# Reordering the first loads of a 64-unit time-mixing kernel: halves on two queues, three units in float32, and a later gate for the casting loads

## The chip, the cores and the metric

The kernel runs on one core of a Trainium2 chip. The metric is device time in microseconds (us) of one execution, lower is better. Each kernel is executed several times; a run with several rounds executes it alternately with the kernel before on the same chip. Medians are quoted. A profile records one execution; its span is about 1.7 to 2.1 us shorter than the time reported for it.

## The reference, cut to what matters

```python
x_prev = np.zeros_like(x); x_prev[:, 1:, :] = x[:, :-1, :]      # x is (16, 2048, 256) float32
xv = x * time_mix_v + x_prev * (1 - time_mix_v)                 # xr likewise; xk and k are not used
v = xv.reshape(-1, 256) @ value_weight
r = xr.reshape(-1, 256) @ receptance_weight
out = (sigmoid(r) * v) @ output_weight                          # float32
```

## The kernel before

The 32,768 rows are worked in 64 units of 512 rows, four units to a batch (of 2048 rows). For each unit TensorE transposes x (`ps_t`), ScalarE copies it to SBUF as bf16 (`xt`), VectorE and GpSimd multiply it by a coefficient per channel (`c_sb`) and VectorE adds the row ahead (`mix`), TensorE projects twice (`psum_r`, `psum_v`), ScalarE takes the sigmoid (`s_sb`), VectorE multiplies (`z_sb`), TensorE does the output product (`psum_o`) and ScalarE copies it out. The weights are multiplied once by `tms` so that the mix needs one product. Transposes run some units ahead, so the order is fixed: while unit 4 is worked on, units 7 and 8 (counted from 0) are transposed as a pair.

How x comes in: GpSimd issues loads that cast float32 to bf16 on the way (`x_bf`). They go through one queue in order. Only the first two units are loaded in float32 by the sync queue (`x_unit`), because that is sooner; they are transposed in float32. A dummy copy on GpSimd that reads a loaded tile is the gate that holds the casting loads back until that tile has landed:

```python
for m, tm in enumerate([time_mix_r, time_mix_v]):
    nc.scalar.dma_start(out=tm_rows[...], in_=...)
nc.scalar.dma_start(out=x_last, in_=rows(0)[:, J - 1, :])
for h in range(2):
    nc.sync.dma_start(out=x_unit[:, 0, h * H : (h + 1) * H], in_=...)
nc.sync.dma_start(out=w_f32[:, 0], in_=...)        # receptance weight
nc.sync.dma_start(out=x_unit[:, 1], in_=...)       # second unit
nc.sync.dma_start(out=w_f32[:, 1], in_=...)        # value weight
...
nc.gpsimd.tensor_copy(out=gate, in_=x_last[:, 0:1])          # gate
load(0, 2 * UJ, 3 * UJ)                                      # third unit, cast
nc.gpsimd.dma_start(out=wo_bf, in_=...)                      # output weight, cast
load(0, 3 * UJ, J)                                           # fourth unit
nc.gpsimd.tensor_copy(out=gate, in_=x_unit[:, 1, 0, 0:1])    # second gate
load(1, 3 * UJ, J); load(1, 0, UJ); load(1, UJ, 3 * UJ)      # second batch
load(2)                                                      # third batch, one load
```

Before the first data TensorE multiplies zeros (34 matmuls, `warm_up(WARM)`; 12 more later) so that its clock comes up: in the profile, four float32 transposes take 1.11 us at 4.93 us and 0.60 us at 6.27.

Of the kernel before, what the change touches and what calls it, by code (L numbers as in the profile page):

```python
# [8 lines left out]
FP32 = mybir.dt.float32  # L9
BF16 = mybir.dt.bfloat16  # L10
ALU = mybir.AluOpType
ACT = mybir.ActivationFunctionType
# [3 lines left out]
def kernel(  # L16
# [22 lines left out]
    nc = tc.nc  # L39

    B, S, D = x.shape
    P = 128
    KO = D // P
    J = S // P
    UJ = 4
    TU = UJ * P
# [3 lines left out]
    H = UJ // 2  # L50
    START_T = [1, 3, 5, 6, 8, 9, 11, 12]
    AHEAD = 6
    PAIRS = 12
    WARM = 34
    WARM2 = 12

    consts = ctx.enter_context(tc.tile_pool(name="consts", bufs=1))
    xpool = ctx.enter_context(tc.tile_pool(name="xpool", bufs=3))
# [4 lines left out]
    ps_t_pool = ctx.enter_context(tc.tile_pool(name="ps_t", bufs=2, space=bass.MemoryType.PSUM))  # L63
    ps_v_pool = ctx.enter_context(tc.tile_pool(name="ps_v", bufs=1, space=bass.MemoryType.PSUM))
    ps_r_pool = ctx.enter_context(tc.tile_pool(name="ps_r", bufs=1, space=bass.MemoryType.PSUM))
# [7 lines left out]
    xt = {}  # L73
    mix = {}
# [5 lines left out]
    ident_f = consts.tile([P, P], FP32)  # L80
# [4 lines left out]
    def rows(b):  # L85
        return x[b].rearrange("(p j) d -> p j d", p=P)

    def load(b, lo=0, hi=J):
        if b not in x_bf:
            x_bf[b] = xpool.tile([P, J, D], BF16, name="x_bf")  # L90
        nc.gpsimd.dma_start(out=x_bf[b][:, lo:hi, :], in_=rows(b)[:, lo:hi, :])  # L91

    x_last = consts.tile([P, D], FP32)
    x_unit = consts.tile([P, 2, UJ, D], FP32)
    tm_rows = consts.tile([2 * KO, P], FP32)
    w_f32 = consts.tile([P, 2, KO, D], FP32)
    for m, tm in enumerate([time_mix_r, time_mix_v]):
        nc.scalar.dma_start(  # L98
            out=tm_rows[m * KO : (m + 1) * KO, :], in_=tm.rearrange("(ko p) -> ko p", p=P)
        )  # L100
    nc.scalar.dma_start(out=x_last, in_=rows(0)[:, J - 1, :])
    for h in range(2):
        nc.sync.dma_start(
            out=x_unit[:, 0, h * H : (h + 1) * H], in_=rows(0)[:, h * H : (h + 1) * H, :]
        )
    nc.sync.dma_start(
        out=w_f32[:, 0], in_=receptance_weight.rearrange("(ko p) n -> p ko n", p=P)
    )
    nc.sync.dma_start(out=x_unit[:, 1], in_=rows(0)[:, UJ : 2 * UJ, :])
    nc.sync.dma_start(out=w_f32[:, 1], in_=value_weight.rearrange("(ko p) n -> p ko n", p=P))  # L110
    sig0 = consts.tile([P, 1], BF16)
    nc.scalar.activation(out=sig0, in_=zeros[:, 0:1], func=ACT.Sigmoid)  # L112
    w_bf = consts.tile([P, 2, KO, D], BF16)
    wo_bf = consts.tile([P, KO, D], BF16)
    gate = consts.tile([P, 1], FP32)
    nc.gpsimd.tensor_copy(out=gate, in_=x_last[:, 0:1])
    load(0, 2 * UJ, 3 * UJ)
    nc.gpsimd.dma_start(out=wo_bf, in_=output_weight.rearrange("(ko p) n -> p ko n", p=P))  # L118
    load(0, 3 * UJ, J)
    nc.gpsimd.tensor_copy(out=gate, in_=x_unit[:, 1, 0, 0:1])  # L120
    load(1, 3 * UJ, J)
    load(1, 0, UJ)
    load(1, UJ, 3 * UJ)
# [6 lines left out]

    warm_up(WARM)

# [5 lines left out]
    tms = consts.tile([P, 2, KO], FP32)  # L138
    c_sb = consts.tile([P, 2, KO], FP32)

    def coefficients():
        ps = ps_o_pool.tile([P, 2, KO], FP32, name="psum_o")
        nc.tensor.transpose(  # L143
            out=ps.rearrange("p m k -> p (m k)"), in_=tm_rows, identity=ident_f[: 2 * KO, : 2 * KO]
        )
        tm = consts.tile([P, 2, KO], FP32)
        nc.vector.tensor_copy(out=tm, in_=ps)  # L147
        nc.vector.tensor_scalar(
            out=tms, in0=tm, scalar1=0.0, scalar2=1e-30, op0=ALU.is_equal, op1=ALU.mult
        )  # L150
        nc.vector.tensor_tensor(out=tms, in0=tms, in1=tm, op=ALU.add)
        nc.vector.reciprocal(c_sb, tms)
        nc.vector.tensor_scalar(out=c_sb, in0=c_sb, scalar1=-1.0, scalar2=None, op0=ALU.add)

    coefficients()

    def transposes(i):

        b, e = divmod(i, UB)
        if b > 0:  # L160
            if e == 0:
                new_xt(b)
            e = (e - 1) % UB
        c0 = (1 + e * UJ) * P
        if i == 1:
            ps = ps_o_pool.tile([P, KO, TU], FP32, name="psum_o")
            src, idn = x_unit[:, 1], ident_f
        else:
            ps = ps_t_pool.tile([P, KO, TU], BF16, name="ps_t")
            src, idn = x_bf[b][:, e * UJ : (e + 1) * UJ, :], ident  # L170
        for ko in range(KO):
            for jj in range(UJ):
                nc.tensor.transpose(  # L173
                    out=ps[:, ko, jj * P : (jj + 1) * P],
                    in_=src[:, jj, ko * P : (ko + 1) * P],
                    identity=idn,
                )
        nc.scalar.copy(out=xt[b][:, :, c0 : c0 + TU], in_=ps)  # L178
        if e == UB - 1:
            late_copies.append(b)  # L180

    def first_transposes():
        def half(h, pool, name):
            ps = pool.tile([P, KO, TU], FP32, name=name)
            for ko in range(KO):
                for jj in range(H):
                    nc.tensor.transpose(  # L187
                        out=ps[:, ko, jj * P : (jj + 1) * P],
                        in_=x_unit[:, 0, h * H + jj, ko * P : (ko + 1) * P],
                        identity=ident_f,  # L190
                    )
            c0 = (1 + h * H) * P
            nc.scalar.copy(out=xt[0][:, :, c0 : c0 + H * P], in_=ps[:, :, 0 : H * P])  # L193

        half(0, ps_r_pool, "psum_r")
        pl = ps_t_pool.tile([P, KO, P], FP32, name="ps_t")
        for ko in range(KO):
            nc.tensor.transpose(
                out=pl[:, ko, 0:P], in_=x_last[:, ko * P : (ko + 1) * P], identity=ident_f
            )  # L200
        nc.vector.tensor_copy(out=xt[0][:, :, 1:P], in_=pl[:, :, 0 : P - 1])
        half(1, ps_v_pool, "psum_v")

    def scale(piece, kos=(0, 1)):
        b, m, lo, hi = piece
        for ko in kos:
            nc.vector.tensor_scalar(  # L207
                out=mix[b][:, m, ko, lo:hi],
                in0=xt[b][:, ko, lo:hi],
                scalar1=c_sb[:, m, ko : ko + 1],  # L210
                scalar2=None,
                op0=ALU.mult,
            )
# [13 lines left out]
    def add(piece):  # L227
        b, m, lo, hi = piece
        return nc.vector.tensor_tensor(  # L229
            out=mix[b][:, m, :, lo:hi],  # L230
            in0=mix[b][:, m, :, lo:hi],
            in1=xt[b][:, :, lo + P : hi + P],
            op=ALU.add,
        )
# [71 lines left out]
    def tile_for(b):  # L306
        if b not in mix:
            mix[b] = mixpool.tile([P, 2, KO, J * P], BF16, name="mix")

    def pieces(g):  # L310

        b, e = divmod(g, UB)
        tile_for(b)
        return [(b, m, e * TU, (e + 1) * TU) for m in range(2)]
# [16 lines left out]
    def advance(limit):  # L331
        nonlocal tnext
        while tnext <= min(limit, NU - 1):
            b, e = divmod(tnext, UB)
            if e == 1 and 2 < b + 2 < B:
                load(b + 2)
            transposes(tnext)
            tnext += 1

    first_transposes()  # L340
    tile_for(0)
    for h in range(2):
        half = (0, 0, h * H * P, (h + 1) * H * P)
        scale(half)
        add(half)
    for ko in range(KO):
        nc.scalar.activation(
            out=w_bf[:, 0, ko, :], in_=w_f32[:, 0, ko, :], func=ACT.Copy, scale=tms[:, 0, ko : ko + 1]
        )
    scale(pieces(0)[1])  # L350
    add(pieces(0)[1])
    for ko in range(KO):
        nc.vector.tensor_scalar(
            out=w_bf[:, 1, ko, :],
            in0=w_f32[:, 1, ko, :],
            scalar1=tms[:, 1, ko : ko + 1],
            scalar2=None,
            op0=ALU.mult,
        )
    warm_up(WARM2)  # L360
    advance(1)
    scale(pieces(1)[0])
    add(pieces(1)[0])

# [18 lines left out]
    for u in range(2, NU):  # L383
# [3 lines left out]
        for m, (b, _, lo, hi) in enumerate(pieces(u)):  # L387
            w = first[u][m]
# [3 lines left out]
                pooled[w - 1].append(group)  # L392
            else:
                products[w].append((group, (0, 1)))

    def scale_act(piece, kos):
        b, m, lo, hi = piece
        for ko in kos:
            nc.scalar.activation(  # L399
                out=mix[b][:, m, ko, lo:hi],  # L400
                in_=xt[b][:, ko, lo:hi],
                func=ACT.Copy,
                scale=c_sb[:, m, ko : ko + 1],
            )

    z_prev = None
    for g in range(NU - 1):
# [5 lines left out]
        for p in products.get(g + 1, []):  # L413
            if g + LOOK >= NU and p[0][1] == 1:
                scale_act(p[0], (0,))
# [57 lines left out]
```

## Time and profile before

| kernel before | |
|---|---|
| median | 213.88 us (213.71 to 214.05, 3 runs) |
| profiled execution | 214.59 us, span 212.8 us |
| busy share TensorE, VectorE, ScalarE, GpSimd | 95, 91, 88, 36 per cent |
| TensorE after 47 us | 3.04 us a unit, no gap |
| fourth unit's cast load | lands at 14.53 us |
| third batch's cast load | lands at 24.8 us |

The shares are averages over stages with different limits, and TensorE's says little about a change in the first 10 us. To value such a change one follows how its gain travels: the first units, then a stretch in which VectorE sets the pace (20 to 47 us), then one in which TensorE does.

### The profile page before, as it was taken

To read this page: it belongs to the slowest core of one execution; us is meant where nothing else is said; L and a number is where in the kernel's file an instruction comes from. 1 tells how busy PE (TensorE), PEld (TensorE's weight loads), DVE (VectorE), ACT (ScalarE), POOL (GpSimd) and SP (SyncE) were. 2 spreads that over 40 slices of the span, in tenths; PEclk is the share of its full clock that TensorE was granted. 3 is DMA by queue.
4 is the path that set the end of the run, shared out by engine and by line. 5 is a ranking of instruction groups with operands and counts; after the bars stand their busy time and mean duration, and the time that the engine had idled before them with its cause. 6 is when DMAs were issued, how large, how long until landed. Compare 5 with 4: busy or idle time off the path is not lost.

```text
span 212.8 us, 4177 instructions
## 1 busy us (share of the span) xinstructions
PE 202.0 (95%) x1566; PEld 134.9 (63%) x1593; DVE 193.8 (91%) x311; ACT 186.9 (88%) x202; POOL 77.1 (36%) x104
## 2 busy tenths in 40 slices
PE   8879999999999999999999999999999999999990
PEld 7537676666666666666666666666666666665570
DVE  1899999999999999999999999998999999999971
ACT  2688999998999999999999999999999999999870
POOL 1802331344453435434452444335343442344200
PEclk9999999999999999999999999999999999999998
DMA  5899999999969989998989999898989944443565
GB/s 181 196 176 216 240 288 285 326 234 337 245 152 288 277 228 339 176 348 179 291 243 225 340 200 354 157 325 211 260 283 216 354 200 197 197 172 162 208 249 200
DMA packets 9340, 51.91 MB, mean 244 GB/s; under 512 B 996, under 2 KB 1896, under 8 KB 3688
## 3 DMA queue, kind: packets, MB, share of 16 engines
q0 software_dynamic: 3008, 16.39, 43.9%
q1 hardware_dynamic: 6016, 34.87, 40.0%
q10 hardware_dynamic: 296, 0.40, 0.5%
q8 instruction: 12, 0.20, 0.3%
q14 instruction: 8, 0.07, 0.1%
HBM read 34.47 MB, written 33.55 MB: 320 GB/s over the span
## 4 chain that ended last, share of the span: by engine, by line
PE 73%; DVE 11%; DMA 5%; ACT 4%; issue 4%; POOL 1%; ACTq 0%; DVEq 0%
PE psum_o L250 22%; PE psum_v L240 20%; PE psum_r L240 19%; PE ps_t L173 10%; DVE z_sb L432 4%; DVE mix L229 3%; DMA x_bf<-in_x_dram 3%; DVE mix L207 2%; ACT s_sb L411 2%; DMA x_last<-in_x_dram 2%; ACT xt L178 1%; ACT o_sb L270 1%; PE ps_t L240 0%; ACTq L98 0%; POOL wo_bf L118 0%
## 5 line engine op out<-in xcount | busy, mean ns | idle before, releaser
L217 POOL TENSOR_SCALAR mix<-xt,c_sb 128x1024 bf16<-128x1024 bf16 (+1 forms) x61 | 64.4, 1057 | 117.0 <-DVE mix L229 101.4
L229 DVE TENSOR_TENSOR mix<-mix,xt 128x1024 bf16<-128x1024 bf16 (+1 forms) x129 | 90.0, 700 | 3.0 <-DVE mix L207 0.5
L432 DVE TENSOR_TENSOR z_sb<-s_sb,psum_v 128x1024 bf16<-128x1024 bf16 x63 | 76.6, 1216 | 4.8 <-PE psum_v L240 2.6
L270 ACT COPY o_sb<-psum_o 128x1024 f32<-128x1024 f32 x62 | 62.9, 1015 | 13.6 <-PE psum_o L250 13.2
L240 PEld LDWEIGHTS <-w_bf 128*128 128x128 bf16 x520 | 48.2, 98 | 35.4 <-issue 1.9
L240 PE MATMUL psum_v<-mix,w_bf 128*128 128x512 bf16 (+1 forms) x241 | 63.9, 377 | 1.7 <-DVE z_sb L432 0.6
L411 ACT ACTIVATE s_sb<-psum_r 128x1024 bf16<-128x1024 f32 x63 | 65.1, 1033 | 0.1
L250 PE MATMUL psum_o<-wo_bf,z_sb 128*128 128x256 bf16 x500 | 64.9, 273 | 0.2
L240 PE MATMUL psum_r<-mix,w_bf 128*128 128x512 bf16 (+1 forms) x244 | 64.0, 377 | 0.5
L178 ACT COPY xt<-ps_t 128x1024 bf16<-128x1024 bf16 x62 | 63.0, 1024 | 0.9 <-PE ps_t L173 0.9
L250 PEld LDWEIGHTS <-z_sb 128*128 128x128 bf16 x512 | 50.0, 98 | 19.1
L173 PEld LDWEIGHTS <-x_bf 128*128 128x128 bf16 x496 | 32.4, 98 | 15.6 <-DMA x_bf<-in_x_dram 2.4
L173 PE MATMUL ps_t<-ident,x_bf 128*128 128x128 bf16 x496 | 37.2, 219 | 1.6 <-DMA x_bf<-in_x_dram 1.4
L207 DVE TENSOR_SCALAR mix<-xt,c_sb 128x1024 bf16<-128x1024 bf16 (+2 forms) x89 | 35.5, 423 | 0.2
L91 POOL DMA_DIRECT2D x_bf<-in_x_dram x19 | 10.9, 577 | 0.0
L129 PE MATMUL ps_t<-zeros 128*128 128x128 bf16 x46 | 4.6, 289 | 1.0 <-DVE zeros L79 1.0
L129 PEld LDWEIGHTS <-zeros 128*128 128x128 bf16 x46 | 4.3, 135 | 1.0 <-DVE zeros L79 1.0
L399 ACT ACTIVATE mix<-xt,c_sb 128x512 bf16<-128x512 bf16 (+1 forms) x4 | 3.6, 930 | 0.0
L147 DVE COPY tm<-psum_o 128x4 f32<-128x4 f32 x1 | 0.2, 161 | 3.5 <-PE psum_o L143 3.5
L325 DVE COPY xt<-xt 128x254 bf16<-128x254 bf16 x15 | 3.3, 218 | 0.0
L112 ACT ACT_TABLE_LOAD x1 | 1.3, 1283 | 2.0 <-issue 2.0
L193 ACT CAST xt<-psum_r 128x512 bf16<-128x512 f32 x1 | 0.6, 585 | 2.5 <-PE psum_r L187 2.5
(45 smaller groups left out, 22.5 us busy)
## 6 DMA issues: line engine op xcount, KB each, us to landing
out_dram<-o_sb SPq DMA_DIRECT2D x30, 1024.0 KB, 7.1
x_bf<-in_x_dram POOLq DMA_DIRECT2D x14, 1024.0 KB, 10.8
x_bf<-in_x_dram POOLq DMA_DIRECT2D x4, 256.0 KB, 7.2
out_dram<-o_sb SPq DMA_DIRECT2D x2, 512.0 KB, 2.6
out_dram<-o_sb SPq DMA_DIRECT2D x3, 256.0 KB, 2.1
x_unit<-in_x_dram SPq DMA_DIRECT2D x2, 256.0 KB, 3.9
x_unit<-in_x_dram SPq DMA_DIRECT2D x1, 512.0 KB, 5.6
x_bf<-in_x_dram POOLq DMA_DIRECT2D x1, 512.0 KB, 10.9
```

The lines of the kernel that those rows point to most:

```text
L91: nc.gpsimd.dma_start(out=x_bf[b][:, lo:hi, :], in_=rows(b)[:, lo:hi, :])
L129: nc.tensor.matmul(out=ps, lhsT=zeros, rhs=zeros, start=True, stop=True)
L173: nc.tensor.transpose(out=ps[:, ko, jj * P : (jj + 1) * P], in_=src[:, jj, ko * P : (ko + 1) * P], identity=idn,)
L178: nc.scalar.copy(out=xt[b][:, :, c0 : c0 + TU], in_=ps)
L207: nc.vector.tensor_scalar(out=mix[b][:, m, ko, lo:hi], in0=xt[b][:, ko, lo:hi], scalar1=c_sb[:, m, ko : ko + 1], scalar2=None, op0=ALU.mult,)
L217: op = nc.gpsimd.tensor_scalar(out=mix[b][:, m, 1, lo:hi], in0=xt[b][:, 1, lo:hi], scalar1=c_sb[:, m, 1:2], scalar2=1.0, op0=ALU.mult, op1 ...
L229: return nc.vector.tensor_tensor(out=mix[b][:, m, :, lo:hi], in0=mix[b][:, m, :, lo:hi], in1=xt[b][:, :, lo + P : hi + P], op=ALU.add,)
L240: nc.tensor.matmul(out=ps[:, mo, :], lhsT=w_bf[:, m, ko, mo * P : (mo + 1) * P], rhs=mix[b][:, m, ko, e * TU + lo : e * TU + hi], start=(k ...
L250: nc.tensor.matmul(out=ps[:, slot, :], lhsT=z[:, ko, jj * P : (jj + 1) * P], rhs=wo_bf[:, ko, :], start=(ko == 0), stop=(ko == KO - 1),)
L270: nc.scalar.copy(out=o_sb[b][:, j0 : j0 + UJ, :], in_=ps)
L411: nc.scalar.activation(out=s_sb, in_=ps_r, func=ACT.Sigmoid)
L432: nc.vector.tensor_tensor(out=z_sb, in0=s_sb, in1=ps_v, op=ALU.mult)
```

## The change

Its intent is to have the first units ready sooner: the first unit's halves go out on two queues, the third unit comes in float32 through the faster queues too, the casting loads wait until the second unit has landed so that they don't compete with it, and work is moved between VectorE and ScalarE. Core of the diff:

```diff
-    WARM = 34
-    WARM2 = 12
+    WARM = 32
+    WARM2 = 10
...
+    load_unit(nc.sync, 0, 0, H)
+    load_unit(nc.scalar, 0, H, UJ)
     for m, tm in enumerate([time_mix_r, time_mix_v]):
-        nc.scalar.dma_start(
+        nc.sync.dma_start(
...
-    nc.gpsimd.tensor_copy(out=gate, in_=x_last[:, 0:1])
-    load(0, 2 * UJ, 3 * UJ)
+    load_unit(nc.sync, 2)                       # after the value weight
+    nc.gpsimd.tensor_copy(out=gate, in_=x_unit[:, 1, 0, 0:1])
+    load(0, 3 * UJ, J)
     nc.gpsimd.dma_start(out=wo_bf, ...)
-    load(0, 3 * UJ, J)
-    nc.gpsimd.tensor_copy(out=gate, in_=x_unit[:, 1, 0, 0:1])
...                                             # both weights scaled on ScalarE,
...                                             # half 1 copied by VectorE, x_last by ScalarE,
...                                             # unit 0 mixed whole, unit 2 transposed in float32
```

More of the change, by code (lines that the diff above doesn't have):

```diff
@@ L93, with load_unit, load_weight @@
     x_last = consts.tile([P, D], FP32)
-    x_unit = consts.tile([P, 2, UJ, D], FP32)
+    x_unit = consts.tile([P, 3, UJ, D], FP32)
     tm_rows = consts.tile([2 * KO, P], FP32)
     w_f32 = consts.tile([P, 2, KO, D], FP32)
+    def load_unit(queue, u, lo=0, hi=UJ):
+        queue.dma_start(out=x_unit[:, u, lo:hi], in_=rows(0)[:, u * UJ + lo : u * UJ + hi, :])
+    def load_weight(m, w):
+        nc.sync.dma_start(out=w_f32[:, m], in_=w.rearrange("(ko p) n -> p ko n", p=P))
+    load_unit(nc.sync, 0, 0, H)
+    load_unit(nc.scalar, 0, H, UJ)
     for m, tm in enumerate([time_mix_r, time_mix_v]):
-        nc.scalar.dma_start(
+        nc.sync.dma_start(
             out=tm_rows[m * KO : (m + 1) * KO, :], in_=tm.rearrange("(ko p) -> ko p", p=P)
@@ L101 @@
     nc.scalar.dma_start(out=x_last, in_=rows(0)[:, J - 1, :])
-    for h in range(2):
-        nc.sync.dma_start(
-            out=x_unit[:, 0, h * H : (h + 1) * H], in_=rows(0)[:, h * H : (h + 1) * H, :]
-        )
-    nc.sync.dma_start(
-        out=w_f32[:, 0], in_=receptance_weight.rearrange("(ko p) n -> p ko n", p=P)
-    )
-    nc.sync.dma_start(out=x_unit[:, 1], in_=rows(0)[:, UJ : 2 * UJ, :])
-    nc.sync.dma_start(out=w_f32[:, 1], in_=value_weight.rearrange("(ko p) n -> p ko n", p=P))
+    load_weight(0, receptance_weight)
+    load_unit(nc.sync, 1)
+    load_weight(1, value_weight)
+    load_unit(nc.sync, 2)
     sig0 = consts.tile([P, 1], BF16)
@@ L145, in coefficients @@
         )
-        tm = consts.tile([P, 2, KO], FP32)
-        nc.vector.tensor_copy(out=tm, in_=ps)
         nc.vector.tensor_scalar(
-            out=tms, in0=tm, scalar1=0.0, scalar2=1e-30, op0=ALU.is_equal, op1=ALU.mult
+            out=tms, in0=ps, scalar1=0.0, scalar2=1e-30, op0=ALU.is_equal, op1=ALU.mult
         )
-        nc.vector.tensor_tensor(out=tms, in0=tms, in1=tm, op=ALU.add)
+        nc.vector.tensor_tensor(out=tms, in0=tms, in1=ps, op=ALU.add)
         nc.vector.reciprocal(c_sb, tms)
         nc.vector.tensor_scalar(out=c_sb, in0=c_sb, scalar1=-1.0, scalar2=None, op0=ALU.add)
-    coefficients()
     def transposes(i):
@@ L164, in transposes, with one @@
         c0 = (1 + e * UJ) * P
+        def one(ps, ko, src, idn):
+            for jj in range(UJ):
+                nc.tensor.transpose(
+                    out=ps[:, jj * P : (jj + 1) * P],
+                    in_=src[:, jj, ko * P : (ko + 1) * P],
+                    identity=idn,
+                )
+        if i == 2:
+            for ko in range(KO):
+                ps = ps_t_pool.tile([P, TU], FP32, name="ps_t")
+                one(ps, ko, x_unit[:, i], ident_f)
+                nc.scalar.copy(out=xt[b][:, ko, c0 : c0 + TU], in_=ps)
+            return
         if i == 1:
             ps = ps_o_pool.tile([P, KO, TU], FP32, name="psum_o")
-            src, idn = x_unit[:, 1], ident_f
+            src, idn = x_unit[:, i], ident_f
         else:
@@ L171, in transposes @@
         for ko in range(KO):
-            for jj in range(UJ):
-                nc.tensor.transpose(
-                    out=ps[:, ko, jj * P : (jj + 1) * P],
-                    in_=src[:, jj, ko * P : (ko + 1) * P],
-                    identity=idn,
-                )
+            one(ps[:, ko], ko, src, idn)
         nc.scalar.copy(out=xt[b][:, :, c0 : c0 + TU], in_=ps)
@@ L182, in first_transposes @@
     def first_transposes():
-        def half(h, pool, name):
+        for h, (pool, name) in enumerate([(ps_r_pool, "psum_r"), (ps_v_pool, "psum_v")]):
             ps = pool.tile([P, KO, TU], FP32, name=name)
@@ L192, in half @@
             c0 = (1 + h * H) * P
-            nc.scalar.copy(out=xt[0][:, :, c0 : c0 + H * P], in_=ps[:, :, 0 : H * P])
-        half(0, ps_r_pool, "psum_r")
+            copy = nc.vector.tensor_copy if h else nc.scalar.copy
+            copy(out=xt[0][:, :, c0 : c0 + H * P], in_=ps[:, :, 0 : H * P])
+            if h == 0:
+                coefficients()
         pl = ps_t_pool.tile([P, KO, P], FP32, name="ps_t")
@@ L200, in first_transposes @@
             )
-        nc.vector.tensor_copy(out=xt[0][:, :, 1:P], in_=pl[:, :, 0 : P - 1])
-        half(1, ps_v_pool, "psum_v")
+        nc.scalar.copy(out=xt[0][:, :, 1:P], in_=pl[:, :, 0 : P - 1])
     def scale(piece, kos=(0, 1)):
@@ L338, in advance, with scale_act, weight_act @@
             tnext += 1
-    first_transposes()
-    tile_for(0)
-    for h in range(2):
-        half = (0, 0, h * H * P, (h + 1) * H * P)
-        scale(half)
-        add(half)
-    for ko in range(KO):
-        nc.scalar.activation(
-            out=w_bf[:, 0, ko, :], in_=w_f32[:, 0, ko, :], func=ACT.Copy, scale=tms[:, 0, ko : ko + 1]
-        )
-    scale(pieces(0)[1])
-    add(pieces(0)[1])
-    for ko in range(KO):
-        nc.vector.tensor_scalar(
-            out=w_bf[:, 1, ko, :],
-            in0=w_f32[:, 1, ko, :],
-            scalar1=tms[:, 1, ko : ko + 1],
-            scalar2=None,
-            op0=ALU.mult,
-        )
+    def scale_act(piece, kos):
+        b, m, lo, hi = piece
+        for ko in kos:
+            nc.scalar.activation(
+                out=mix[b][:, m, ko, lo:hi],
+                in_=xt[b][:, ko, lo:hi],
+                func=ACT.Copy,
+                scale=c_sb[:, m, ko : ko + 1],
+            )
+    def weight_act(m):
+        for ko in range(KO):
+            nc.scalar.activation(
+                out=w_bf[:, m, ko, :], in_=w_f32[:, m, ko, :], func=ACT.Copy, scale=tms[:, m, ko : ko + 1]
+            )
+    first_transposes()
+    unit0 = pieces(0)
+    weight_act(0)
+    scale(unit0[0])
+    scale(unit0[1], (0,))
+    add(unit0[0])
+    scale(unit0[1], (1,))
+    add(unit0[1])
     warm_up(WARM2)
     advance(1)
+    weight_act(1)
     scale(pieces(1)[0])
@@ L394 @@
                 products[w].append((group, (0, 1)))
-    def scale_act(piece, kos):
-        b, m, lo, hi = piece
-        for ko in kos:
-            nc.scalar.activation(
-                out=mix[b][:, m, ko, lo:hi],
-                in_=xt[b][:, ko, lo:hi],
-                func=ACT.Copy,
-                scale=c_sb[:, m, ko : ko + 1],
-            )
     z_prev = None
```

## The prediction

> **What bounds the kernel now.** I read the shares of the page first, then busy time by stage, then the chain of waits, and then the first 20 us in order of time. The columns of the stage table are the stretch, its length, busy us of each engine with instruction counts, the granted clock, the DMA share and GB/s:
>
> ```profile
> 0.00:10.00 10.00, 8.48 (x68) 6.98 (x69) 4.51 (x18) 4.46 (x7) 4.67 (x15) 1.00 0.69 194
> 10.00:20.00 10.00, 8.03 (x66) 4.93 (x67) 9.07 (x20) 8.24 (x11) 1.73 (x4) 1.00 1.08 189
> 20.00:47.00 27.00, 26.61 (x218) 17.80 (x221) 27.00 (x53) 26.11 (x29) 8.05 (x14) 1.00 1.02 268
> 47.00:205.00 158.00, 156.45 (x1197) 103.40 (x1218) 150.67 (x219) 146.06 (x155) 62.65 (x72) 1.00 0.83 248
> ```
>
> From 47 us on TensorE has no gap. The chain there is made of its groups alone: 0.86 + 0.86 + 0.87 + 0.45 = 3.04 us a unit. From 20 to 47 us VectorE is busy for all 27.00 us, TensorE and ScalarE nearly so; the chain runs through z_sb (L432), the adds (L229) and the products (L207). The change touches neither stretch: below the second unit its instruction lists are those of before. What it can do is start them earlier. A shift of VectorE at 20 us passes one for one to the end, because both stretches follow in order and TensorE has about 1.2 us of stalls to give between 16.8 and 48.4 us (29.15 us of groups in the 29.81 us between two r projections, then 0.56 us before L240 at 48.45). So the question is what sets the start. The chain of waits, in start, us, what:
>
> ```profile
> 1.59 4.35 DMA x_last<-in_x_dram
> 6.18 0.66 POOL x_bf L91
> 6.84 0.70 POOL wo_bf L118
> 7.55 6.98 DMA x_bf<-in_x_dram
> 14.58 0.62 PE ps_t L173 x8
> 15.20 0.86 PE psum_v L240 x4
> 16.06 0.89 PE psum_o L250 x8
> 16.97 1.01 ACT o_sb L270
> 17.98 0.92 ACT s_sb L411
> 18.91 1.83 ACT xt L178 x2
> ```
>
> x_last lands at 5.94 us and opens the cast loads; the fourth unit's cast load (third in the queue) lands at 14.53; TensorE, then ScalarE, carry that to 20.74 us, where VectorE takes over. The lines of the same time show the rest (start, us, engine, line, what, idle before and releaser):
>
> ```profile
> 7.90 1.06 PE L173 MATMUL psum_o<-ident_f,x_unit 128*128 128x128 f32 x8 [0.36 <-DMA x_unit<-in_x_dram]
> 9.07 1.02 PE L240 MATMUL psum_r<-mix,w_bf 128*128 128x512 bf16 x3
> 10.64 1.08 PE L240 MATMUL psum_v<-mix,w_bf 128*128 128x512 bf16 x4 [0.54 <-DVE w_bf L353]
> 12.20 0.62 PE L173 MATMUL ps_t<-ident,x_bf 128*128 128x128 bf16 x8 [0.49 <-DMA x_bf<-in_x_dram]
> 14.58 0.62 PE L173 MATMUL ps_t<-ident,x_bf 128*128 128x128 bf16 x8 [0.89 <-DMA x_bf<-in_x_dram]
> 16.17 1.22 DVE L432 TENSOR_TENSOR z_sb<-s_sb,psum_v 128x1024 bf16<-128x1024 bf16 x1 [0.53 <-PE psum_v L240]
> 19.66 1.22 DVE L432 TENSOR_TENSOR z_sb<-s_sb,psum_v 128x1024 bf16<-128x1024 bf16 x1 [0.28 <-PE psum_v L240]
> ```
>
> TensorE loses 2.49 us between 9.07 and 16.77 us (7.70 us, in which its groups need 5.21), on the second weight and two cast loads. But VectorE, the later bound, waits only 0.53 and 0.28 us. That caps the gain well below 2.49.
>
> **What the Trainium skill says.** "DMA: Bandwidth & Descriptors", section "Issuing engines are not separate DMA queues": queues of several engines share the 16 DMA engines, so a second issuer saves only issue time. The trace agrees in kind: the sync queue took 0.86 us for two halves; they landed 3.2 and 4.6 us after issue. The same page, "SWDGE vs HWDGE vs iDMA", says that a load that casts must be issued by GpSimd; that is why the change has to take the third unit in float32. Its section "Anatomy of one DMA" gives about 2.0 us of fixed time, mostly the receipt. The trace agrees: the cast queue had moved 0.655 MB, all through the fourth unit, by about 12.9 us, and that load landed at 14.53, 1.6 us later. "ScalarE: Activation LUTs", section "What ACT_TABLE_LOAD costs", gives 280 ns plus 0.833 ns a column with one pointer operand, and 93 ns of overlap back to back: 493 ns for 256 columns. The trace has 497 to 510, and 0.91 us for two.
>
> **The change part by part.** Times are of the new kernel, estimated from durations of the old trace.
>
> 1. Front. 32 warm matmuls at 112 ns instead of 34 end at about 4.6 us, not 4.8. The halves leave on two queues; the second lands near 4.5 instead of 5.8. Four first transposes at the cold pace of about 0.24 us a step run to 5.55. The coefficients follow (not first): matrix at 5.8, four small VectorE operations instead of five at 0.2 us, to 6.6. Half 1 is copied by VectorE: 254 columns from PSUM took 0.42 us and 1024 took 1.21, so 512 cost about 0.69, to 7.3. ScalarE copies half 0 to 6.25, the x_last columns to 7.25, and scales the r weight to 8.15. VectorE: two products and one of v, 0.9 us, the add 0.65: r mix ready at 8.85 (before: 8.92). The whole-unit products and adds cost 0.67 + 0.69 = 1.36 us where two halves cost 0.61 + 0.42 + 0.48 + 0.42 = 1.93, but 0.69 came in and 0.42 went: a wash. First projection 8.9 instead of 9.07.
>
> 2. Second unit. Its transposes wait for x_unit, which landed at 7.8. The bytes ahead in the queue are the same and start 0.4 us earlier, but two issues of time_mix stand ahead: 7.5 to 7.8 us. Its copy on ScalarE starts at 8.5 to 8.95; I use 8.95.
>
> 3. v weight on ScalarE: two at 0.41 us step, after that copy, so 9.9 to 10.7. v projection from 10.35, its second half at 10.75, as before; the sigmoid of unit 0 moves from 10.13 to 10.7 and ends 11.75. VectorE loses 0.67 us of work; z of unit 0 starts at 11.75 instead of 12.00, now behind the sigmoid.
>
> 4. Third unit in float32: eight transposes in 1.06 us instead of 0.62 and two copies at 0.585 instead of one of 1.01, both beside other work. Data at about 9 us (0.52 MB at 400 GB/s behind the rest). TensorE takes it straight after the v projection, at 11.5 to 12.6, instead of waiting to 12.20. ScalarE: scaled v of unit 1 11.65 to 12.97, copies 12.9 to 13.9, sigmoid of unit 1 to 14.9. VectorE: z to 12.95, add to 13.6, four products to 14.85, add to 15.5. z of unit 1 at 15.5 instead of 16.17; with the 1.14 + 2.07 us of work up to the next, z of unit 2 at 18.7 instead of 19.66. Gain so far 0.95 us.
>
> 5. Cast loads. The gate moves from 5.94 to about 7.7, but 0.26 MB of the old stream (unit 2) is gone and unit 3 goes first. First packets came 1.6 us after the issue: 9.4. The old stream moved 128 packets of 2 KB in about 1.8 us, then 256 short ones of the output weight in about 1.6: unit 3 moved at 11.2 and landed at 12.9 (before 14.53), output weight moved at 12.9. At 12.9 us the old stream stood at exactly this point, so everything behind lands as before. The DMA engines have no spare time there (share 1.08). Those landings: fifth and sixth unit about 16.0 and 17.3 (bytes moved by 14.3 and 15.7 us, plus the 1.6), third batch 24.8 us (issued 9.93, 14.9 us to landing).
>
> 6. So the gain meets the third batch. The ninth unit's transposes came second of a pair starting at 24.37, thus at 24.82 us, just as the data landed. A TensorE 0.95 us ahead must wait there; v of that step then ends at 24.8 + 0.45 + 0.86 + 0.1 = 26.2, and z, which ran at 26.49, moves by only 0.25 to 0.3 us. If the stream is 0.2 to 0.5 us ahead of mine, as it is when x_unit lands at 7.4, 0.5 to 0.8 remain. I take 0.45 us.
>
> **Rivals.** (a) The whole 0.95 us or more survives, if x_unit lands by 7.3 (earlier issue of the halves speaks for it) so that copies, gate and stream all move: about 212.8. Against it speaks a DMA share of 1.0 from 11 to 47 us. (b) Nothing gained: the 1.8 us later gate and 0.26 MB more float32 reading delay the fifth to ninth unit; 17.3 for the sixth leaves at most 0.1 us against its new turn. Half a microsecond of later landing makes it 214.1. (c) ScalarE, with 0.84 us more work before the first sigmoid (0.95 for the weight, 0.42 for x_last, less 0.58), becomes the bound. Summing its steps from 8.95 to the copies of units 4 and 5 gives 10.4 us, so 19.4 against 20.74 before. It is close, but does not bind unless its start slips by over 1 us: 214.0. (d) The TensorE clock falls back in the shorter warm-up; the two trims are four instructions, 0.4 us, so at worst some 0.2 us.
>
> **Range and chances.** 213.88 less 0.45 is 213.43; I say 213.4. Range 212.7 to 214.3: rival (a) at one end, and (b) with run-to-run spread of 0.2 us at the other. Two per cent is 4.28 us, more than all TensorE stalls after 9 us that the start can cause, and slower by that would need a stalled stream; each gets 0.01.
>
> **What would show it right or wrong.** TensorE should start the third unit's transposes directly after v of unit 0, with no wait for x_bf at 12 us, and the fourth unit's before 13.7 us. z of unit 0 should name the sigmoid. z of unit 2 should start near 18.7. The ninth unit's transposes should show a new wait for x_bf near 24 us. From 49 us on all rows should be the old ones, shifted. Wrong: x_unit later than 8 us, fourth unit after 14 us, or a gap on VectorE between 20 and 47 us that isn't behind the third batch.

## The result, and the profile after

The changed kernel took 215.88 us in the median (215.25 to 216.21, 4 runs) against 213.80 us (213.60 to 214.05, 4 runs). Ratios here are the mean time of one kernel's fast runs over that of the other's of the same rounds, so not quite the ratio of the medians: 1.0092, with a 95% interval of 1.0072 to 1.0112. Executions over 1.5% slower than the fastest of the same kernel are left out of the means. The predicted range ended at 214.3; the forecast gain of 0.45 us is a loss of 2.1.

The profiled execution of the changed kernel is its fastest (215.25 us, span 213.2), that of the kernel before a slow one. So the two traces differ by only 0.4 us in span and show where the loss arises better than how large it is. Stage table of the changed kernel, same columns as in the prediction:

```profile
0.00:10.00 10.00, 7.04 (x62) 6.17 (x64) 3.45 (x13) 3.88 (x7) 2.52 (x10) 1.00 0.71 225
10.00:20.00 10.00, 9.29 (x70) 5.83 (x71) 9.28 (x18) 9.38 (x14) 3.17 (x7) 1.00 1.06 175
20.00:47.00 27.00, 25.93 (x214) 17.25 (x215) 26.24 (x52) 25.52 (x28) 8.04 (x14) 1.00 1.02 266
47.00:205.00 158.00, 156.42 (x1197) 103.21 (x1217) 150.99 (x220) 145.95 (x155) 62.65 (x72) 1.00 0.83 249
```

The first 10 us hold less VectorE work than before (3.45 us, 4.51 before). From 10 to 20 us VectorE and ScalarE are busier, as intended. But from 20 to 47 us VectorE, full before, has lost 0.76 us, and that stretch passes its losses on to the end. The last row is the old one. The chain of waits (start, us, what) says what VectorE lacked:

```profile
2.30 5.83 DMA x_unit<-in_x_dram
8.12 0.05 issue
8.18 0.18 POOL gate L120
8.36 0.66 POOL x_bf L91
9.03 0.72 POOL wo_bf L122
9.74 1.59 POOL x_bf L91 x3
11.34 14.14 DMA x_bf<-in_x_dram
...
25.53 0.62 PE ps_t L166 x8
```

Second unit, gate, GpSimd's issues one after the other, then the third batch's cast load from 11.34 to 25.48 us. It used to be issued at 9.93 and to land at 24.8. Now the lines in order of time that answer to those of before, and after them unit 8 in the kernel before, inside a pair without a wait:

```profile
5.85 0.63 PE L195 MATMUL psum_r<-ident_f,x_unit 128*128 128x128 f32 x4 [1.26 <-DMA x_unit<-in_x_dram]
8.26 1.06 PE L166 MATMUL psum_o<-ident_f,x_unit 128*128 128x128 f32 x8 [0.27 <-DMA x_unit<-in_x_dram]
9.77 1.02 PE L248 MATMUL psum_r<-mix,w_bf 128*128 128x512 bf16 x3 [0.44 <-DVE mix L237]
11.89 1.04 PE L166 MATMUL ps_t<-ident_f,x_unit 128*128 128x128 f32 x8
12.16 1.22 DVE L435 TENSOR_TENSOR z_sb<-s_sb,psum_v 128x1024 bf16<-128x1024 bf16 x1 [0.21 <-ACT s_sb L414]
14.33 0.62 PE L166 MATMUL ps_t<-ident,x_bf 128*128 128x128 bf16 x8 [0.54 <-DMA x_bf<-in_x_dram]
19.46 1.22 DVE L435 TENSOR_TENSOR z_sb<-s_sb,psum_v 128x1024 bf16<-128x1024 bf16 x1 [0.33 <-PE psum_v L248]
25.53 0.62 PE L166 MATMUL ps_t<-ident,x_bf 128*128 128x128 bf16 x8 [0.75 <-DMA x_bf<-in_x_dram]
```

```profile
24.37 1.10 PE L173 MATMUL ps_t<-ident,x_bf 128*128 128x128 bf16 x16
```

Two things are to be seen. The first transposes start at 5.85 us after 1.26 us of waiting for the first half; before they started at 4.93. And at 25.53 us there is a wait that the kernel before did not have: unit 8, second of its pair, waits 0.75 us for the third batch. The z of unit 2 still ran 0.2 us earlier than before (19.46 against 19.66); the projection at 49.08 us ran 0.63 us later than its counterpart at 48.45. The loss lies between, at that wait.

### The profile page after: what moved, and what is told of

Its sections match the earlier page's. It is cut to its first block, busy times and chain, and to the rows that moved or that the text cites. A ratio compares the mean times of both kernels' runs of the same rounds, so it can differ in the third digit from the quotient of the medians.

```text
span 213.2 us, 4166 instructions
## 1 busy us (share of the span) xinstructions
PE 201.7 (95%) x1562; PEld 134.8 (63%) x1589; DVE 192.7 (90%) x305; ACT 187.4 (88%) x205; POOL 76.4 (36%) x102
## 4 chain that ended last, share of the span: by engine, by line
PE 72%; DMA 9%; DVE 9%; issue 4%; ACT 1%; POOL 1%; SPq 1%; DVEq 0%
PE psum_o L258 22%; PE psum_v L248 20%; PE psum_r L248 19%; PE ps_t L166 10%; DMA x_bf<-in_x_dram 7%; DVE mix L237 3%; DVE z_sb L435 3%; DMA x_unit<-in_x_dram 3%; DVE mix L215 2%; ACT s_sb L414 1%; POOL x_bf L91 1%; PE ps_t L248 0%; POOL wo_bf L122 0%; DVE o_sb L311 0%; SPq L107 0%
## 5 line engine op out<-in xcount | busy, mean ns | idle before, releaser
L237 DVE TENSOR_TENSOR mix<-mix,xt 128x1024 bf16<-128x1024 bf16 x128 | 89.4, 701 | 2.6
L186 ACT COPY xt<-ps_t 128x1024 bf16<-128x1024 bf16 x61 | 62.1, 1026 | 0.0
L215 DVE TENSOR_SCALAR mix<-xt,c_sb 128x1024 bf16<-128x1024 bf16 (+1 forms) x87 | 35.2, 428 | 0.1
L91 POOL DMA_DIRECT2D x_bf<-in_x_dram x18 | 10.4, 583 | 0.0
```

Source lines behind the costliest of these rows:

```text
L91: nc.gpsimd.dma_start(out=x_bf[b][:, lo:hi, :], in_=rows(b)[:, lo:hi, :])
L186: nc.scalar.copy(out=xt[b][:, :, c0 : c0 + TU], in_=ps)
L215: nc.vector.tensor_scalar(out=mix[b][:, m, ko, lo:hi], in0=xt[b][:, ko, lo:hi], scalar1=c_sb[:, m, ko : ko + 1], scalar2=None, op0=ALU.mult,)
L237: return nc.vector.tensor_tensor(out=mix[b][:, m, :, lo:hi], in0=mix[b][:, m, :, lo:hi], in1=xt[b][:, :, lo + P : hi + P], op=ALU.add,)
```

## The experiments

Theory A: the later gate delays the stream of casting loads, and the third batch's late landing sets the end. Theory B: the two halves on two queues share the DMA engines, both land late, and the late front is what costs. Theory C came up from the first traces: TensorE falls idle before the late half, and in some executions its clock then stays low. "Low clock" here means matmuls and transposes that take about twice as long; the granted-clock column reads 1.00 there, so it is read from the durations alone. Ratios are to the kernel before of the same call; its medians were 214.10, 214.10, 214.18 and 214.17 us in the four calls. Each kernel had 6 executions and its results were correct.

### The changed kernel again

No edit.

> The changed kernel unaltered, on the chip of the next three, for a second trace and as their baseline. If the loss of 2.1 us in the timed runs is of the kernel and not of one chip: ratio to the kernel before 1.007 to 1.011, about 215.8 us. If the third batch's late landing is the cause (theory A), the trace again shows a wait of TensorE for x_bf of 0.7 us or more near 24 to 26 us. If the sharing of DMA engines by the first two halves is the cause (theory B), the first transposes again start after 5.6 us (4.9 before).

Measured: 215.61 us (215.24 to 215.96), ratio 1.0057 [1.0032, 1.0081]. The loss repeats, at 1.5 us here. The trace was a surprise:

```profile
5.41 1.09 PE L195 MATMUL psum_r<-ident_f,x_unit 128*128 128x128 f32 x4 [0.82 <-DMA x_unit<-in_x_dram]
9.03 1.61 PE L166 MATMUL psum_o<-ident_f,x_unit 128*128 128x128 f32 x8
10.47 1.03 PE L248 MATMUL psum_r<-mix,w_bf 128*128 128x512 bf16 x3
24.93 1.06 PE L166 MATMUL ps_t<-ident,x_bf 128*128 128x128 bf16 x16
```

There is no wait for x_bf anywhere; the expectation of theory A failed for this execution. Instead four transposes take 1.09 us (0.63 in the first trace) and the second unit's eight take 1.61 (1.06): the array runs slowly until about 10 us, and the first projection starts at 10.47 instead of 9.77. Unit 8's transposes come up 0.45 us into the pair that starts at 24.93, at 25.38 us, when the data is already there. So the same kernel reaches the same end by two ways: a late third batch, or a slow front that arrives no earlier than the batch does. The two run side by side and do not add.

### The gate back on x_last

```diff
-    nc.gpsimd.tensor_copy(out=gate, in_=x_unit[:, 1, 0, 0:1])
+    nc.gpsimd.tensor_copy(out=gate, in_=x_last[:, 0:1])
```

> The changed kernel with the gate of the cast loads back on x_last, as before; everything else of the change kept. Theory A (the later gate delays the whole cast stream, and TensorE waits for the third batch): the third batch lands at 23.5 to 24.5 us, the wait near 25 us is gone, and the time falls by 1.2 to 2.5 us, to 213.3 to 214.6. Theory B (the first halves land late): no change, 215.5 to 216.2, or slower, because the cast loads now share the engines with the second unit's load.

Measured: 213.71 us (213.42 to 214.39), ratio 0.9971 [0.9946, 0.9995]; 1.9 us less than the changed kernel on the same chip. The third batch landed at 24.59, and unit 8 waited 0.32 us in the profiled execution, the slowest of the six:

```profile
24.64 0.62 PE L166 MATMUL ps_t<-ident,x_bf 128*128 128x128 bf16 x8 [0.32 <-DMA x_bf<-in_x_dram]
```

Theory A holds for size and place, though the batch landed 0.1 us after the expected 23.5 to 24.5 and a short wait was left. B falls as the cause of the loss: the front is as late as ever (first transposes at 5.77 us).

### The halves back on one queue

```diff
-    load_unit(nc.scalar, 0, H, UJ)
+    load_unit(nc.sync, 0, H, UJ)
...
-        nc.sync.dma_start(out=tm_rows[...
+        nc.scalar.dma_start(out=tm_rows[...
```

> The changed kernel with the two first halves and the time_mix rows back on the queues of before; gate and the rest as changed. Theory B: first transposes start at about 4.7 us instead of 5.85, the whole start moves up by about 0.6 us, second unit and gate too, and the time falls by 1 us or more, to under 214.9. Theory A: the first transposes start earlier but the second unit's landing (8.1 us) and so the gate and the third batch hardly move: 215.4 to 216.2.

Measured: 215.59 us (215.22 to 217.58), ratio 1.0070 [1.0036, 1.0105]: no gain. The front moved, the end did not:

```profile
4.38 0.90 PE L195 MATMUL psum_r<-ident_f,x_unit 128*128 128x128 f32 x4
26.54 0.62 PE L166 MATMUL ps_t<-ident,x_bf 128*128 128x128 bf16 x8 [0.94 <-DMA x_bf<-in_x_dram]
```

The first transposes start 1.5 us sooner than in the first trace of the changed kernel, so theory B is right that two queues cost the first half its early landing. But the second unit landed no sooner (8.44 us), which left only 0.29 us of the lead at the first projection (9.48 against 9.77); the gate opened then, and the third batch landed at 26.49. The early first half was worth nothing.

Over the traces in which unit 8 waited for its data, TensorE's last product ended a constant time after that start: 25.53 and 208.03 us in the changed kernel (182.50), 24.64 and 207.16 with the old gate (182.52), 26.54 and 209.05 here (182.51). What delays that start delays the end one for one. The constant alone does not show that the landing is the limit: it is 182.57 us where unit 8 did not wait (24.82 and 207.39 us in the kernel before). That takes the wait, and the next run, which removes it.

### The third batch's load cut in two

```diff
-    load(2)
+    load(2, 3 * UJ, J)
+    load(2, 0, 3 * UJ)
```

> The changed kernel with the third batch's cast load cut in two, its last quarter (whose transposes come first) as a load of its own ahead of the other three. Theory A: that quarter lands about 2.5 us earlier, near 22.5 us, the wait near 25 us is gone, and at least 0.6 us come back: 213.6 to 215.3. Theory B: the time stays at 215.5 to 216.2.

Measured: 214.37 us (213.27 to 215.92), ratio 1.0005 [0.9966, 1.0043]; 1.2 us better than the changed kernel with the gate still late. The wait at unit 8 was gone from the trace (0.96 us at unit 3's weight loads and 0.19 us at unit 5 are left), and TensorE ended at 207.17 us. The landing of unit 8's data was thus a real limit. The spread of 2.6 us shows that something else still varied.

### A longer warm-up

```diff
-    WARM = 32
+    WARM = 42
```

> The changed kernel with 42 warm matmuls ahead of the first transposes instead of 32, so that TensorE works until about 5.7 us, when the first half lands. Theory A (late cast stream alone): the wait for the third batch stays, 215.3 to 216.0 us, no faster than the changed kernel. Theory C (the trimmed warm-up lets TensorE fall idle and its clock stays low until 10 us in some executions, which is where the rest of the loss comes from): median down by 0.4 us or more, below 215.2, and a profile with no first-stage transposes at 1.1 us for four.

Measured: 215.12 us (214.53 to 215.80), ratio 1.0047 [1.0028, 1.0066]. The front was at full clock in the trace (first projection at 9.18 us), and unit 8 then waited 0.98 us and started at 25.53. Down by about half a microsecond against the changed kernel's run in another call, just under the bound of 215.2 set for C, with a spread that overlaps: weak support for C. The trace shows that with the late gate a quicker front mostly waits longer at unit 8.

### Old gate and the cut load

> The changed kernel with the gate on x_last and the third batch's load cut in two. Theory A with the start of the third batch's transposes setting the end (end of TensorE = that start + 182.5 us in three traces): without that wait VectorE sets the pace from its own start, z of unit 2 at about 19.0 us as in the run with the old gate; 212.8 to 213.5 us, faster than either part alone. If the third batch was already harmless with the old gate: 213.5 to 214.0, as with the gate alone.

Measured: 214.31 us (213.71 to 215.03), ratio 1.0004 [0.9982, 1.0027]. Not faster than either part: expectation missed. The six times fall in two groups, 213.71, 213.77, 213.88 and 214.74, 214.75, 215.03. The profiled execution is of the slower group:

```profile
5.70 1.09 PE L196 MATMUL psum_r<-ident_f,x_unit 128*128 128x128 f32 x4 [1.11 <-DMA x_unit<-in_x_dram]
10.49 1.02 PE L249 MATMUL psum_r<-mix,w_bf 128*128 128x512 bf16 x4 [0.29 <-DVE mix L238]
```

No wait for x_bf at all, and the slow front of the repeated run again. With the stream no longer in the way, the slow clock is fully visible: it costs about 1 us in this execution (first projection at 10.49 us, 9.38 in the trace of the second old-gate run below).

### Only the gate, in the kernel before

```diff
-    nc.gpsimd.tensor_copy(out=gate, in_=x_last[:, 0:1])
+    nc.gpsimd.tensor_copy(out=gate, in_=x_unit[:, 1, 0, 0:1])
     load(0, 2 * UJ, 3 * UJ)
...
-    nc.gpsimd.tensor_copy(out=gate, in_=x_unit[:, 1, 0, 0:1])
```

> The kernel before with nothing changed but the gate: all cast loads wait for the second unit. Theory A: third and fourth unit land later by the 1.8 us of the gate, and so does the third batch, now behind 0.26 MB more than in the changed kernel: 215.5 to 217.5 us and waits for x_bf near 12, 14 and 26 us. Theory B or C: the gate is nearly free, 213.8 to 214.6.

Measured: 216.35 us (215.57 to 217.10), ratio 1.0102 [1.0079, 1.0126]. The gate alone makes the kernel before 2.2 us slower. Units 2 and 3 now start at 13.06 and 17.09 us after 1.30 and 1.29 us of waiting:

```profile
13.06 1.03 PE L172 MATMUL ps_t<-ident,x_bf 128*128 128x128 bf16 x8 [1.30 <-DMA x_bf<-in_x_dram]
```

What the gate takes is DMA time: between 8 and 9 us the DMA share is 0.01, against 0.90 in the kernel before. The array's clock even fell back meanwhile: eight transposes from 13.06 us took 1.03 us, 0.62 from 17.09, and here the granted-clock column shows it (0.50 from 14 to 16 us). As TensorE then waited 1.29 us for unit 3 anyway, that should have cost little. In this kernel the later gate already bites at units 2 and 3; no wait showed up to 27 us beyond them.

### Old gate, cut load and longer warm-up

> Gate on x_last, third batch's load cut in two, 42 warm matmuls. Theory C: no execution with the low clock, so a narrower spread (under 0.6 us from lowest to highest) and a median at or below that of the run without the longer warm-up, 212.6 to 213.3. If the clock never mattered: the same median as without it within 0.2 us, or 0.1 to 0.2 us later because the warm matmuls stand in front of the first transposes.

Measured: 213.81 us (213.22 to 214.56), ratio 0.9987 [0.9969, 1.0005]. Half a microsecond below the same kernel with the short warm-up; the median missed the expected range, 212.6 to 213.3, by 0.5 us, and the spread, 1.3 us, is as wide as without it, so theory C's expectation failed on both counts. The trace has no wait for x_bf, the first projection at 8.94 us, z of unit 2 at 18.45, and TensorE's end at 206.18.

### A version meant to beat both

Old gate, cut load, halves and time_mix rows on their old queues, `WARM = 34`, `WARM2 = 18`.

> A version meant to beat both: the changed kernel with the gate on x_last, the third batch's load cut in two, the first halves and time_mix rows on the queues of before, 34 and 18 warm matmuls so that TensorE is never idle for long before 9 us. Theories A and C together: no wait for x_bf between 9 and 27 us, TensorE at full clock from 6 us on, first projection near 9.3 us because the second unit lands at about 8.3 us with this order; 212.8 to 213.6 us, ratio to before 0.993 to 0.998. If the second unit's landing is what now sets the start: 213.6 to 214.2.

Measured: 214.02 us (213.55 to 215.24), ratio 0.9986 [0.9951, 1.0021]. The first transposes ran at 4.48 us and full clock, but the second unit's began only at 8.77, after 1.72 us of waiting for its load. This order gives the first half an early landing and takes it back from the second unit, and the time lies in the range expected if that landing sets the start.

### The cut load in the kernel before

> The kernel before with only the third batch's load cut in two. In its trace that load landed at the very moment its transposes came up, 24.8 us, and TensorE did not wait; the cut should give nothing on average and at most remove the slower executions: 213.6 to 214.2 us, ratio 0.998 to 1.001. A ratio under 0.997 would say that the third batch already limited the kernel before.

Measured: 214.01 us (213.82 to 214.38), ratio 0.9980 [0.9947, 1.0012]. As expected: in the median the third batch is not a limit of the kernel before that can be seen. Unit 8 starts at about 24.1 us in this trace, 0.7 us ahead of the slow execution on record.

### A shorter warm-up in the kernel before

```diff
-    WARM = 34
+    WARM = 20
```

> The kernel before with 20 warm matmuls instead of 34, so that TensorE idles from about 3.3 to 4.7 us as the changed kernel idles from 4.6 to 5.8. Theory C: in some executions the clock stays low to about 10 us; the twelve first transposes and the second unit's then take about twice as long (+1.2 us of TensorE time before the first projection), median 214.3 to 215.2 us and a wider spread. If the clock does not matter: 213.7 to 214.3.

Measured: 213.91 us (213.87 to 214.40), ratio 0.9979 [0.9949, 1.0009]. The strong form of theory C falls here, and the trace shows why:

```profile
8.04 1.55 PE L173 MATMUL psum_o<-ident_f,x_unit 128*128 128x128 f32 x8
9.42 1.03 PE L240 MATMUL psum_r<-mix,w_bf 128*128 128x512 bf16 x4
13.54 0.62 PE L173 MATMUL ps_t<-ident,x_bf 128*128 128x128 bf16 x8 [0.43 <-DMA x_bf<-in_x_dram]
```

The clock was low until past 8 us (1.55 us for eight transposes), the first projection came at 9.42. Yet TensorE still had to wait for unit 3's data at 13.54 us, and 0.28 us for the third batch at 24.23, so the margin of the kernel before is small there too. In the kernel before a slow front hides behind the casting loads. It costs only where those are not in the way.

### The gate moved further

```diff
-    nc.gpsimd.tensor_copy(out=gate, in_=x_unit[:, 1, 0, 0:1])
+    nc.gpsimd.tensor_copy(out=gate, in_=x_unit[:, 2, 0, 0:1])
```

> The changed kernel with the gate moved further, onto the third unit, which lands near 10.5 to 11 us: a larger dose of the suspected cause. Theory A: fourth unit and third batch land about 2.5 us later than in the changed kernel; TensorE waits for x_bf near 14 us and near 26 to 28 us, and the time rises by 1.5 to 2.7 us, to 217.3 to 218.5. If the gate is not what counts: under 216.2.

Measured: 218.04 us (217.17 to 221.10), ratio 1.0178 [1.0128, 1.0227]. A larger dose of the suspected cause gives a larger loss: 3.9 us over the kernel before, where the changed kernel lost 2.1 and 1.5, so about 2 us more. One of the six executions, 221.10, is slow; another, 220.35, is far out too. While this gate was shut the DMA engines stood still (share 0.02 from 10 to 11 us, 0.00 from 11 to 12), and the third batch landed at 28.32. Two new waits of this trace:

```profile
15.89 0.62 PE L166 MATMUL ps_t<-ident,x_bf 128*128 128x128 bf16 x8 [2.01 <-DMA x_bf<-in_x_dram]
18.24 1.03 PE L258 MATMUL psum_o<-wo_bf,z_sb 128*128 128x256 bf16 x8 [0.87 <-DMA wo_bf<-in_output_weight_dram]
```

### Old gate with and without the longer warm-up

It was still open why the rest of the change gains so little with the old gate.

> The changed kernel with the gate on x_last and 42 warm matmuls, the third batch's load whole. If the trimmed warm-up costs something once the cast loads are early (theory C in its weaker form): 212.9 to 213.5 us, below the run with the gate alone in the same call by 0.3 us or more. If not: within 0.2 us of it.

> The changed kernel with the gate on x_last alone, a second time, as the candidate that beats both kernels: ratio to before 0.995 to 0.999 as in its first run (0.9971), and a trace in which the wait for the third batch near 24.6 us is under 0.5 us. A ratio of 1.000 or more would take the gain over the kernel before back, though not that over the changed kernel.

Measured: 213.81 us (213.39 to 214.53), ratio 0.9982 [0.9967, 0.9997], with 42 warm matmuls (expected 212.9 to 213.5); 214.89 us (213.80 to 215.18), ratio 1.0027 [1.0012, 1.0042], with 32. The gain of the gate alone over the kernel before did not repeat; that over the changed kernel did, smaller. Beside each other the two differ by 1.08 us, and their intervals do not overlap. The times with 32 are again one near 213.8 (the profiled one, at full clock), one at 214.30, and four from 214.82 to 215.18, the slower group of the cut-load run. Its first run had none of that group. With 42 no time lies in that group, though 214.53 comes close, as did 214.56 in the earlier run with 42. Lines of the run with 42:

```profile
5.67 0.63 PE L195 MATMUL psum_r<-ident_f,x_unit 128*128 128x128 f32 x4 [0.74 <-DMA x_unit<-in_x_dram]
23.72 1.06 PE L166 MATMUL ps_t<-ident,x_bf 128*128 128x128 bf16 x16
```

Full clock from the first transposes on, and unit 8's data on time. That the slow group is the low clock is seen in one profiled execution of it (the cut-load run) and in the repeated run; for the other executions it is inferred from their times. The kernel before has executions up to 215.93 us too, whose cause no trace shows, so this part is argued more than shown.

## Why the prediction was wrong, point by point

**What bounds the kernel: right.** VectorE passes a shift between 20 and 47 us on to the end, and TensorE's stretch after 47 us is the old one, moved.

**Step 1, the front: wrong on the landing.** It let the second half land near 4.5 us and took the first to be there when 32 warm matmuls end at 4.6. In the traces of the changed kernel the first transposes start at 5.85 and 5.41 us, waiting for the first half. Both halves, issued at 0.74 us on two queues, took 5.0 and 5.2 us to land; one behind the other they took 3.2 and 4.6 before. The page I quoted says that the queues share the engines. I read it as "no gain" and did not draw the other conclusion, that the piece needed first loses what the second wins. The clock then followed: **rival (d)** had the low clock at "at worst some 0.2 us". It costs about 1 us once the casting loads are no longer in the way: 1.11 us at the first projection between two traces with the old gate, 1.08 between the medians with 32 and 42 warm matmuls.

**Steps 2 to 4, the parts on ScalarE and VectorE: right in kind.** Second unit at 8.1 us (7.5 to 7.8 predicted), r mix ready at 9.71 instead of 8.85 and so the first projection at 9.77, z of unit 0 behind the sigmoid at 12.16 (11.75), third unit's transposes straight after the v projection at 11.89 (11.5). With old gate and full clock (the run with cut load and longer warm-up) z of unit 2 ran at 18.45; the prediction said 18.7. That agreement is partly luck: 19.66, from which the gain of 0.95 us was reckoned, is of a slow execution, and two traces of the kernel before with a small edit (cut load, shorter warm-up), on another chip, have 18.97 and 18.62. Two sums were off, without effect: ScalarE's added work in rival (c) is 0.95 + 0.42 - 0.58 = 0.79 us, not 0.84, and the "wash" of step 1 saves 0.30 us.

**Step 5, the casting loads: the step that failed.** "So everything behind lands as before" was the sentence. The gate opened at 8.18 instead of 7.7, the first packets moved at about 9.9 instead of 9.4, and unit 3 landed at 14.3 instead of 12.9. The stream's bytes, counted in bf16, were 0.36 MB at 13 us where I had 0.39. But the third batch landed at 25.48, 0.68 us late, in the fastest execution. Two of the prediction's own signs of being wrong were there: the second unit came after 8 us and the fourth after 14, and the wait for the fourth left z of unit 2 only 0.2 us early instead of 0.95. The part that can be named is the gate: it hangs on the second unit, which landed at 8.13, and the stream started 0.5 us later than forecast. The third unit's float32 load was not in the way: queue 1 had moved 1.83 of its 1.84 MB by 10 us, and the DMA share from 9 to 10 us was 0.45. What the gate took away at the start was not given back. From 13 to 18 us the stream fell somewhat further behind, at about the same DMA share; why stays open. Nor does the gate alone fix the landing: in the one-queue run it opened 0.3 us later than in the changed kernel and the third batch landed 1.0 us later.

**Step 6, the gain meets the third batch: right mechanism.** The wait came at unit 8, at the place named. The term that was mis-sized is the landing, put at 24.8 at the latest and found at 25.48 (twice) and 26.49 us in the three traces with the changed kernel's gate in which unit 8 waited. And 24.8 was itself late: in the run with the shorter warm-up the kernel before had the batch at 24.17. That would explain why 0.68 us between the two traces goes with 2.1 us between the medians. By the constant 182.5 us to the end of TensorE, plus about 5.2 us to the end of the span, the changed kernel's spans of 213.2 to 214.2 us would mean starts of unit 8 between 25.5 and 26.5; that is an estimate, as only two of those executions have a trace.

**Rival (b), a late stream, was the right one, and its size was wrong:** "half a microsecond of later landing makes it 214.1". With the gate back the loss of about 2 us goes away (1.9 us in the first call; 0.7 by medians of different calls in its second run, where the slow group was frequent); the gate alone costs 2.2 us in the kernel before, and a further gate about 2 us more. With both faults removed there is a gain near the forecast: 213.81 against 214.17 us, 0.36 us (ratio 0.9982 [0.9967, 0.9997]), where 0.45 had been predicted for the whole change. That the sizes are alike is luck, as the forecast let the third batch eat half of a larger gain. The earlier run with both faults removed and the load cut is 0.29 us below the kernel before, not clear of noise. No run undid the third unit's float32 load or the work moved between VectorE and ScalarE, so what these are worth alone is not known.

## What to carry to other kernels

A gate that keeps bulk loads from competing with urgent ones can cost time wherever the bulk is used just in time, here 17 us later; before moving it, list for each load behind it when it lands and when it is needed, and give the piece needed first a load of its own. Splitting an urgent transfer over two queues made both parts land late here (5.0 and 5.2 us after issue, against 3.2 and 4.6 on one queue), so the part needed first lost its lead. A delay that one wait hides (here the slow clock behind the casting loads) appears in full when that wait is removed, so with two parallel limits the worth of removing one shows fully only when the other is gone too. And a prediction built on one profile should ask first whether that execution was a typical one.

## What the Trainium skill lacked or had wrong

- "DMA: Bandwidth & Descriptors", section "Issuing engines are not separate DMA queues": it says that the transfers interleave and what a second issuing engine saves. It gives no figure for what the piece needed first loses: two 256 KB halves landed 5.0 and 5.2 us after issue on two queues, 3.2 and 4.6 us on one.
- The same page has no rate for loads that cast. In the kernel before their stream went from 0.50 to 2.98 MB of bf16 between 12 and 24 us, 0.21 MB a us. That is twice as much float32 read, about 413 GB/s; the float32 loads moved 409 and 353 GB/s from 5 to 7 us at a like DMA share (1.09 and 0.97). So here a casting load cost the engines about what it read, not what it wrote.
- "TensorE: Matmul & The Clock Gate", section "Part 1: The HAM clock gate (the "warmup" mystery)", says that the activity window runs free and that the transition varies by about 500 ns from run to run under sustained matmuls. It has no figure for a warm-up that ends in a gap: in the changed kernel, after a gap of 1.3 us behind the zero matmuls the array was fast at 5.85 us in one execution, after one of 0.8 us slow until about 10 us in another; about 1 us of the total hung on it.
